# Piece-contiguous weight layout, later caching of the first mixer's weights, a skewed first norm, and LN statistics and a conv tap on ScalarE

## The chip, the cores and the metric

The kernel runs on 8 cores of one Trainium2 chip. Each core works on its own 4096 of the 32768 tokens, and the cores do not talk to one another. The metric is device time in microseconds (us) of the slowest core. Engines are named as in the profile: PE (TensorE matmul), PEld (its weight loads), DVE (VectorE), ACT (ScalarE), POOL (GpSimd), SP (SyncE, which here only issues DMA).

Executions come in two states. In the fast state the times of one kernel mostly lie within some tenths of a per cent. In the slow state the cores of one die, or of both, show a lower granted clock, and the run is per cents longer.

## The reference, cut to what matters

```python
# Layer 0: RMSNorm -> one input projection, split between mixer A and mixer B
z = h @ w_in                                   # 1024 -> 2560 columns
a = a_val * sigmoid(a_gate)                    # A: gated linear unit
a = causal_depthwise_conv(a, conv_a_w) + conv_a_b      # 31 taps, 512 channels
a = silu(layer_norm(a, ln_a_g, ln_a_b))        # LN over the 512 channels
bo = b_gate * causal_depthwise_conv(c_gate * b_val, conv_b_w)   # B: 3 taps
h = h + concatenate([a, bo]) @ w_out           # 1024 -> 1024
h = h + squared_relu_mlp(rms_norm(h), w1, w2)  # 1024 -> 4096 -> 1024
# Layer 1: a gMLP mixer, then another squared-ReLU MLP; at the end a final RMSNorm
```

Inputs and weights are float32. The kernel computes its matmuls in bfloat16.

## The kernel before: the parts that the argument touches

Each core runs four macro tiles (called tiles 0 to 3 below) of 1024 tokens through both layers. "Mixer 0" is layer 0's mixer, "mixer 1" layer 1's. The weights pass through the core as 45 *pieces* of 1024x512 per tile, in a ring of four 1 MB slots. In tile 0 a piece is read from DRAM in float32 and cast to bfloat16 by the DMA (2 MB read, 1 MB written, issued by POOL). When its last reader is done with the slot, the bfloat16 piece is stored to a DRAM cache (1 MB, issued by ACT). Tiles 1 to 3 load all pieces from the cache (1 MB, ACT's queue).

```python
def issue(i, gate=()):
    ...
    if i >= NPIECE:                                    # tiles 1 to 3: from the cache
        src = wcache[i % NPIECE].rearrange("p (kc n) -> p kc n", kc=8)
        P.op("act", lambda e, s=s, src=src: e.dma_start(out=ring[s][:], in_=src),
             reads=[("wc", i % NPIECE)], writes=[("w", s)], dma=f"v{s}")
        return
    src = W[wn][r0:r0 + 1024, c0:c0 + 512].rearrange("(kc p) n -> p kc n", p=128)
    P.op("pool", lambda e, s=s, src=src: e.dma_start(out=ring[s][:], in_=src),   # casts
         reads=list(gate), writes=[("w", s)], dma=f"w{s}")
```

Mixer 0 needs its data in another partition layout twice. The output of A's gated unit goes through a DRAM scratch, `scr_a`, into the tile `A4` that feeds the convolution (four stores of 256 KB and four reloads, issued by SP). The result after LN goes through `scr_s` into `mixT`, which feeds the output projection. The convolution runs on PE against expanded weights `cw`, which `gen_cw` builds on DVE during tile 0's first matmuls. LN's statistics are a matmul with ones and six small operations; then, per block m of four, POOL subtracts the mean, DVE multiplies by the inverse deviation, ACT applies SiLU, and SP stores.

```python
small("dve", lambda e: e.tensor_scalar(out=ln_mean.v, in0=banks[b][:, 0:TP], scalar1=1.0 / 512, ...))
small("dve", lambda e: e.tensor_scalar(out=ln_t.v, in0=banks[b][:, TP:2 * TP], scalar1=1.0 / 512, ...))
small("dve", lambda e: e.tensor_tensor(out=ln_rstd.v, in0=ln_mean.v, in1=ln_mean.v, op=ALU.mult))      # L832
small("dve", lambda e: e.scalar_tensor_tensor(out=ln_t.v, in0=ln_t.v, scalar=LN_EPS, in1=ln_rstd.v,
                                              op0=ALU.add, op1=ALU.subtract))                          # L834
small("act", lambda e: e.activation(out=ln_rstd.v, in_=ln_t.v, func=AF.Sqrt))
small("dve", lambda e: e.reciprocal(out=ln_rstd.v, in_=ln_rstd.v))
for m in range(4):
    for eng, t_, op in (("pool", ln_mean, ALU.subtract), ("dve", ln_rstd, ALU.mult)):   # L843
        lazy(m, eng, ...)
    ...                                        # SiLU on ACT, store to scr_s[m], two reloads into mixT
```

The first norm of tile 0 runs tile by tile: statistics and reciprocal root, scaling on ACT or DVE in turn, eight transposes on PE, a copy with the norm's gain on DVE (`xnT`), then matmuls. The other norms are hidden behind matmuls of earlier stages.

Of the kernel before, what the change touches and what calls it, by code (L numbers as in the profile page):

```python
# [18 lines left out]
NTB = 8  # L19
NSLOT = 4  # L20
# [163 lines left out]
GRAN = 256  # L184
B_COLS = [("c", 0), ("v", 0), ("c", 1), ("v", 1), ("g", 0), ("c", 2), ("v", 2), ("g", 1), ("c", 3), ("v", 3), ("g", 2), ("g", 3)]
# [30 lines left out]
def build_program(n_mt=4):  # L216
# [4 lines left out]
    W = {  # L221
        "ev_w_in": dram("ev_w_in", [1024, 2560]), "ev_w_out": dram("ev_w_out", [1024, 1024]),
        "od_w_in": dram("od_w_in", [1024, 2048]), "od_w_out": dram("od_w_out", [1024, 1024]),
        "w1_0": dram("w1_0", [1024, 4096]), "w1_1": dram("w1_1", [1024, 4096]),
        "w2_0": dram("w2_0", [4096, 1024]), "w2_1": dram("w2_1", [4096, 1024]),
    }
# [10 lines left out]
    with contextlib.ExitStack() as es:  # L237
# [14 lines left out]
        mhalf = sb("mhalf", [128, 1])  # L252
        st = sb("st", [128, 64])
# [78 lines left out]
        def issue(i, gate=()):  # L332
            if i >= len(pieces):
                return
            assert i == issued[0]
            issued[0] += 1
            wn, r0, c0 = pieces[i]
            s = i % NSLOT
            if i >= NPIECE:
                src = wcache[i % NPIECE].rearrange("p (kc n) -> p kc n", kc=8)  # L340
                P.op("act", lambda e, s=s, src=src: e.dma_start(out=ring[s][:], in_=src),
                     reads=[("wc", i % NPIECE)], writes=[("w", s)], dma=f"v{s}")
                return
            src = W[wn][r0:r0 + 1024, c0:c0 + 512].rearrange("(kc p) n -> p kc n", p=128)
            P.op("pool", lambda e, s=s, src=src: e.dma_start(out=ring[s][:], in_=src),
                 reads=list(gate), writes=[("w", s)], dma=f"w{s}")

        def take(expect):
# [5 lines left out]
            if i < NPIECE < len(pieces):  # L354
                wb_left[s] = [2, i]
# [4 lines left out]
        def used(s):  # L360
# [3 lines left out]
            if wb_left[s][0] == 0:  # L364
                i = wb_left.pop(s)[1]
                dst = wcache[i].rearrange("p (kc n) -> p kc n", kc=8)
                P.op("act", lambda e, s=s, dst=dst: e.dma_start(out=dst, in_=ring[s][:]),
                     reads=[("w", s)], writes=[("wc", i)], dma=f"wb{s}")
# [16 lines left out]
        def h_keys(tb):  # L385
            return [("h", tb, 0), ("h", tb, 1)]

        P.op("sp", lambda e: e.dma_start(out=sm[:], in_=smallp), writes=[("sm",)], dma="c0")
        issue(0)
        small("pool", lambda e: e.memset(identf.v, 0.0), [], identf.k())  # L390
        small("pool", lambda e: e.affine_select(out=identf.v, in_=identf.v, pattern=[[-1, 128]],
                                                compare_op=ALU.not_equal, fill=1.0, base=0,
                                                channel_multiplier=1), identf.k(), identf.k())
        small("pool", lambda e: e.tensor_copy(out=ident[:], in_=identf.v), identf.k(), [("ident",)])
        small("pool", lambda e: e.memset(mhalf[:], -0.5), [], [("mhalf",)])
        for tb in range(NTB):
            load_x(0, tb)
            if tb == 0:
                P.op("sp", lambda e: e.dma_start(out=wexp.v, in_=wexp_d.rearrange("p (g u) -> p g u", g=NG)),
                     writes=wexp.k(), dma="c1")  # L400
# [11 lines left out]
        def gen_cw(g):  # L412
            small("dve", lambda e: e.tensor_tensor(
# [124 lines left out]
        def norm_to_xnT(nidx):  # L538
# [5 lines left out]
            def tile(tb):  # L544
                if tb + 1 < NTB:
                    stat_tb(c0, tb + 1)
                    rstd_aff(c0, tb + 1)
                rstd_sqrt(c0, tb)
                rstd_rcp(c0, tb)
                xn_op(c0, tb, "act" if tb % 2 == 0 else "dve")  # L550
# [590 lines left out]
```

## Time and profile before

| | before |
|---|---|
| median of three runs | 2734.26 us (2732.64 to 2736.68) |
| PE busy in the profiled execution | 2645.3 of 2730.4 us |
| of the rest: before t = 200, that is in tile 0's mixer 0 | 58.6 us |
| mean granted clock, core 2 | 0.994 |

PE is the bound, and nearly all that can be won by moving work is the PE idle time at the start. These are lines of the page of the profile before: the span, busy time by engine, then the span cut into 40 slices, where each digit is the busy share of one slice in tenths (PEclk is the clock granted to PE, DMA the share of 16 DMA engines), then one DMA queue (packets, MB, share of 16 engines), and one group of DMA issues (count, size, median time to landing).

```profile
span 2730.4 us, 39950 instructions; the slowest of 8 cores (2717.9 to 2730.4 us)
...
PE 2645.3 (97%) x13400; PEld 1260.4 (46%) x13400; DVE 1061.8 (39%) x1957; ACT 907.5 (33%) x1627; POOL 689.0 (25%) x676
...
PE   5889999999999999999999999999999999999998
...
PEclk9989999999999999999999999999999999999999
DMA  8668765887652112123244122123316222212212
...
q0 software_dynamic: 46800, 47.19, 12.5%
...
ring<-wcache ACTq DMA_DIRECT2D x135, 1024.0 KB, 5.7
```

The first four digits of PE are the loss. DMA is busiest in the same first quarter, which is tile 0, where every piece is cast from float32 and stored to the cache. The queue q0 carries those cast loads: 47.19 MB in 46800 packets, about 1 KB each.

The view of waits says what PE waited for, over the whole span (line and tile that PE was about to run, what ended the wait, us in total, times, longest).

```profile
PE bank L500 <- ACT xn_tm L487: 19.8, 2, 16.9
PE bank L631 <- DVE Z L913: 10.9, 4, 2.9
PE bank L631 <- DMA Z<-scr_s: 9.5, 1, 9.5
PE bank L784 <- DMA Z<-scr_a: 8.9, 3, 5.0
...
PE bank L681 <- DVE Z L913: 8.1, 4, 2.3
```

L500 is the transposes of the first norm, L784 the convolution, L631 the output projection, and L913 DVE's multiply by mixer B's gate, which frees a PSUM bank or completes `mixT`. Of the waits on `scr_a` and `scr_s`, 8.9 and 9.5 us, all but 0.55 us lies in tile 0. The two lines with L913 make 19.0 us, or 4.75 us in each of the four mixers 0.

DVE's part of the LN statistics in tile 1, from the timeline of DVE in the kernel before (start, duration, line, operation, destination and source, shapes, count; in brackets the idle time before and what ended it):

```profile
785.31 2.53 DVE L832 TENSOR_TENSOR Z<-Z 128x256 f32<-128x256 f32 x1
787.95 2.38 DVE L834 SCALAR_TENSOR_TENSOR Z<-Z 128x256 f32<-128x256 f32 x1
...
796.77 3.32 DVE L904 SCALAR_TENSOR_TENSOR Z<-Z,sm 128x768 f32<-128x768 f32 x4
```
The timeline of POOL in the same stretch of the kernel before:

```profile
785.21 9.64 POOL L843 TENSOR_TENSOR Z<-Z 128x1024 f32<-128x1024 f32 x4 [10.68 <-DVE Z L828]
```

Two DVE operations on 128x256 elements take 2.53 and 2.38 us. The operations of that size just before them, which read PSUM, take 0.42 and 0.41 us. The two slow ones end as POOL's subtractions end (9.64 us for four, so 2.41 us each, from 785.21 on). The Trainium skill, "SBUF — State Buffer", section "Who interferes with whom", says that a DVE instruction with two SBUF inputs and a GpSimd instruction that reads SBUF cannot run together, and that the one to issue second blocks until the first is done. This trace agrees.

The load on the machine at that time, from the view of windows (stretch, length, busy time with count of PE, PEld, DVE, ACT and POOL, then clock, DMA share, GB/s):

```profile
735.00:765.00 30.00, 30.00 (x152) 14.52 (x150) 11.27 (x18) 7.55 (x14) 0.00 (x0) 1.00 0.70 216
```

The first `scr_a` store of tile 1 was issued at 745.39, and the reload that waits for it at 755.59, so it took 10.2 us. PE was busy for all 30 us, because the matmuls of mixer A covered it.

### The profile page before, as it was taken

The numbers are of one execution on the slowest core, as the hardware profiler recorded it, in microseconds if no ns is written. First come the engines' busy times: TensorE is split into PE (matmuls) and PEld (weight loads), VectorE is DVE, ScalarE is ACT, GpSimd is POOL, SyncE is SP. The second block draws the span as 40 slices with busy tenths as digits, with TensorE's granted clock in tenths as the row PEclk, the third lists the DMA queues.
The fourth block names the chain that finished last, engine by engine and source line by source line (L and its number), as shares of the span: only waits on it lengthen the run. The fifth ranks groups of instructions, "written<-read, shape, count | busy, mean of one in ns | idle before, by whom it ended". The sixth has DMA issues, their size and how long they took to land.

```text
span 2730.4 us, 39950 instructions; the slowest of 8 cores (2717.9 to 2730.4 us)
## 1 busy us (share of the span) xinstructions
PE 2645.3 (97%) x13400; PEld 1260.4 (46%) x13400; DVE 1061.8 (39%) x1957; ACT 907.5 (33%) x1627; POOL 689.0 (25%) x676
## 2 busy tenths in 40 slices
PE   5889999999999999999999999999999999999998
PEld 2434444444454444444454444454445444444443
DVE  3841226422464223731157321561135721265223
ACT  3332126423344114523333312552333422164112
POOL 0115321423212222223301223123320033203222
PEclk9989999999999999999999999999999999999999
DMA  8668765887652112123244122123316222212212
GB/s 163 133 143 163 163 136 124 177 182 144 211 174 74 73 65 89 64 95 122 78 166 143 62 93 78 47 83 119 107 72 209 78 93 78 78 54 86 78 62 93
DMA packets 122407, 303.87 MB, mean 111 GB/s; under 512 B 22880, under 2 KB 85344, under 8 KB 99040
## 3 DMA queue, kind: packets, MB, share of 16 engines
q10 hardware_dynamic: 25920, 188.76, 18.7%
q0 software_dynamic: 46800, 47.19, 12.5%
q1 hardware_dynamic: 49488, 65.38, 7.5%
q8 instruction: 112, 1.84, 0.3%
q14 instruction: 87, 0.71, 0.1%
HBM read 276.13 MB, written 72.35 MB: 128 GB/s over the span
## 4 chain that ended last, share of the span: by engine, by line
PE 90%; DVE 3%; DMA 3%; issue 3%; ACT 0%; SPq 0%; DVEq 0%; ACTq 0%
PE bank L694 43%; PE bank L681 41%; PE bank L500 2%; PE bank L784 2%; PE bank L631 1%; DMA scr_s<-Z 1%; DMA scr_a<-Z 1%; DVE Z L904 1%; PE bank L1014 1%; DMA Z<-scr_a 0%; DMA h<-x 0%; DVE Z L832 0%; DVE Z L834 0%; DVE Z L913 0%; DVE Z L901 0%
## 5 line engine op out<-in xcount | busy, mean ns | idle before, releaser
L681 PE MATMUL bank<-xnT,ring 128*128 128x512 bf16 x5888 | 1292.1, 380 | 13.1 <-DVE Z L913 8.1
L694 PE MATMUL bank<-ring,Z 128*128 128x512 bf16 x4928 | 1080.9, 379 | 0.1
L702 DVE TENSOR_TENSOR h<-bank,h 128x512 f32<-128x512 f32 x640 | 439.5, 690 | 1397.1 <-PE bank L694 1352.3
L681 PEld LDWEIGHTS bank<-xnT,ring 128*128 128x128 bf16 x5888 | 573.6, 98 | 699.2 <-issue 24.6
L733 POOL TENSOR_TENSOR Z<-Z 128x512 bf16<-128x512 f32 x512 | 531.2, 1039 | 1108.2 <-ACT Z L731 1108.1
L694 PEld LDWEIGHTS bank<-ring,Z 128*128 128x128 bf16 x4928 | 479.3, 98 | 565.4 <-issue 0.6
L731 ACT ACTIVATE Z<-bank 128x512 f32<-128x512 f32 x512 | 304.1, 597 | 1109.1 <-PE bank L681 1080.6
L472 ACT ACTIVATE junk<-h 128x1024 bf16<-128x1024 f32 x136 | 141.8, 1043 | 147.5 <-DVE h L702 80.2
L487 ACT ACTIVATE xn_tm<-h,st 128x1024 bf16<-128x1024 f32 x100 | 114.6, 1146 | 116.0 <-DVE st L519 100.5
L512 DVE TENSOR_TENSOR xnT<-bank,sm 128x1024 bf16<-128x1024 bf16 x96 | 115.5, 1216 | 19.1 <-PE bank L500 19.1
L694 PE MATMUL bank<-ring,xnT 128*128 128x512 bf16 x512 | 115.1, 379 | 0.0
L500 PE MATMUL bank<-ident,xn_tm 128*128 128x128 bf16 x928 | 70.7, 223 | 33.0 <-ACT xn_tm L487 19.8
L500 PEld LDWEIGHTS bank<-ident,xn_tm 128*128 128x128 bf16 x928 | 60.4, 99 | 61.5 <-issue 43.6
L986 POOL TENSOR_TENSOR st<-st,mhalf 128x1 f32<-128x1 f32 x32 | 17.6, 549 | 236.5 <-DVE st L984 236.5
L784 PE MATMUL bank<-Z,cw 128*128 128x256 bf16 x576 | 67.2, 280 | 8.9 <-DMA Z<-scr_a 8.9
L694 PEld LDWEIGHTS bank<-ring,xnT 128*128 128x128 bf16 x512 | 49.4, 98 | 56.7
L526 ACT ACTIVATE st<-st 128x1 f32<-128x1 f32 x160 | 31.0, 194 | 130.8 <-DVE st L519 108.7
L1022 DVE SCALAR_TENSOR_TENSOR Z<-bank,sm,biasT 128x128 f32<-128x128 f32 x256 | 68.9, 339 | 12.8 <-PE bank L1014 12.4
L631 PE MATMUL bank<-ring,Z 128*128 128x512 bf16 x192 | 47.2, 409 | 20.4 <-DVE Z L913 10.9
L784 PEld LDWEIGHTS bank<-Z,cw 128*128 128x128 bf16 x576 | 57.6, 100 | 18.8 <-issue 9.9
L1027 POOL TENSOR_TENSOR Z<-Z 128x512 bf16<-128x512 f32 x44 | 50.4, 1158 | 62.7 <-DVE Z L1022 62.7
L968 DVE TENSOR_TENSOR Z<-bank,cst 128x512 f32<-128x512 f32 x64 | 44.1, 689 | 40.2 <-PE bank L694 32.5
(88 smaller groups left out, 983.2 us busy)
## 6 DMA issues: line engine op xcount, KB each, us to landing
ring<-wcache ACTq DMA_DIRECT2D x135, 1024.0 KB, 5.7
wcache<-ring ACTq DMA_DIRECT2D x45, 1024.0 KB, 9.2
h<-x SPq DMA_DIRECT2D x32, 512.0 KB, 11.1
ring<-w_0 POOLq DMA_DIRECT2D x16, 1024.0 KB, 13.9
ring<-w_1 POOLq DMA_DIRECT2D x16, 1024.0 KB, 19.2
y<-Z SPq DMA_DIRECT2D x32, 512.0 KB, 3.1
Z<-x SPq DMA_DIRECT2D x24, 512.0 KB, 6.9
ring<-ev_w_in POOLq DMA_DIRECT2D x5, 1024.0 KB, 16.7
```

The lines of the kernel that those rows point to most:

```text
L472: small("act", lambda e: e.activation(out=junk[:], in_=ap, func=AF.Square, accum_out=st[:, c0 + tb:c0 + tb + 1]), keys, [("st", c0 + tb), ...
L487: small("act", lambda e: e.activation(out=out, in_=ap, func=AF.Copy, scale=col), keys + [("st", c0 + 8 + tb)], okeys)
L500: r = e.transpose(tbk[:, kc * 128:(kc + 1) * 128], xt[:, kc * 128:(kc + 1) * 128], ident[:])
L512: small("dve", lambda e: e.tensor_tensor(out=xnT[:, :, tb * 128:(tb + 1) * 128], in0=tbk.rearrange("p (k n) -> p k n", k=8), in1=gcol.unsq ...
L631: r = e.matmul(banks[b][:], lhsT=lhs(kc, tb), rhs=ring[slot][:, kc, :], start=(kc == 4), stop=(kc == 3))
L681: r = e.matmul(banks[b][:], lhsT=ring[slot][:, kc, m * 128:(m + 1) * 128], rhs=xnT[:, kc, s * 512:(s + 1) * 512], start=(kc == 0), stop=(k ...
L694: r = e.matmul(banks[b][:], lhsT=lhs(kc, tb), rhs=ring[slot][:, kc, :], start=(kc == 0), stop=(kc == 7))
L702: small("dve", lambda e: e.tensor_tensor(out=h[:, tb, d * 512:(d + 1) * 512], in0=banks[b][:], in1=h[:, tb, d * 512:(d + 1) * 512], op=ALU ...
L731: small("act", lambda e, b=b, rb=rb: e.activation(out=rb.v, in_=banks[b][:], func=AF.Relu), [("ps", b)], rb.k())
L733: small("pool", lambda e, rb=rb, hq=hq, c=c, s=s: e.tensor_tensor(out=hq.v[:, c, s * 512:(s + 1) * 512], in0=rb.v, in1=rb.v, op=ALU.mult), ...
L784: r = e.matmul(banks[b][:, half_ * TP:(half_ + 1) * TP], lhsT=cw[:, g, L * 128:(L + 1) * 128], rhs=A4.v[:, g, HB - L:HB - L + TP], start=( ...
L1022: r = e.scalar_tensor_tensor(out=sv.v[:, j * 128:(j + 1) * 128], in0=banks[b][:, j * 128:(j + 1) * 128], scalar=sm[:, SM_LNGV + g:SM_LNGV ...
```

## The change

Five things to shorten the 58.6 us at the start and the small waits in each mixer 0:

1. The host lays each piece out contiguously, so that what a partition gets of it is one run of 16 KB in float32, where it was eight runs of 2 KB. Piece 0 is split into two halves, and the first half is loaded alone, so that the first matmul group can start sooner.
2. The seven pieces of mixer 0 are cached one tile later. Their cache stores leave tile 0 and happen in tile 1, which therefore casts these seven pieces from float32 again.
3. The first norm is skewed: the statistics of a tile run ahead of the scaling of the tile before, all scaling is on ACT, the transposes come one step later, and three of the `gen_cw` go to POOL.
4. In the LN statistics the square goes to ACT, one operation is dropped and one reads PSUM.
5. The last tap of mixer B's 3-tap convolution goes from DVE to ACT, for three of its four blocks.

```diff
+NSPLIT = 1
+NLATE = 7
 ...
-    W = { "ev_w_in": dram("ev_w_in", [1024, 2560]), ... }
+    W = {n: dram(n, [128 * (k // 1024) * (c // 512), 4096]) for n, (k, c) in WSHAPE.items()}
 ...  (issue)
-            if i >= NPIECE:
-                src = wcache[i % NPIECE].rearrange("p (kc n) -> p kc n", kc=8)
-                P.op("act", lambda e, s=s, src=src: e.dma_start(out=ring[s][:], in_=src), ...
+            if i // NPIECE > cache_mt(i):          # cache_mt: 1 for pieces 0 to NLATE-1, else 0
+                P.op("act", lambda e, s=s, i=i: e.dma_start(out=ring_flat(s), in_=wcache[i % NPIECE]), ...
                 return
-            src = W[wn][r0:r0 + 1024, c0:c0 + 512].rearrange("(kc p) n -> p kc n", p=128)
+            q = (r0 // 1024) * (WSHAPE[wn][1] // 512) + c0 // 512
+            src = W[wn][q * 128:(q + 1) * 128, :]
+            if wn == "ev_w_in" and q < NSPLIT:     # two halves, each with its own key
+                ...
 ...  (first norm)
             stats(0)
+            for tb in range(4):
+                stats(tb + 1)
+                scale(tb)
+                if tb > 0:
+                    tr_op(nidx, tb - 1)
+                gen_cw(3 + tb)
+            tr_op(nidx, 3)
 ...  (LN statistics)
-                small("dve", ... out=ln_t.v, in0=banks[b][:, TP:2 * TP], scalar1=1.0 / 512 ...)
-                small("dve", ... out=ln_rstd.v, in0=ln_mean.v, in1=ln_mean.v, op=ALU.mult ...)
-                small("dve", ... out=ln_t.v, in0=ln_t.v, scalar=LN_EPS, in1=ln_rstd.v ...)
-                small("act", ... activation(out=ln_rstd.v, in_=ln_t.v, func=AF.Sqrt) ...)
+                small("act", ... activation(out=ln_t.v, in_=ln_mean.v, func=AF.Square) ...)
+                small("dve", ... scalar_tensor_tensor(out=ln_t.v, in0=banks[b][:, TP:2 * TP], scalar=1.0 / 512,
+                                                      in1=ln_t.v, op0=ALU.mult, op1=ALU.subtract) ...)
+                small("act", ... activation(out=ln_rstd.v, in_=ln_t.v, func=AF.Sqrt, bias=leps[:, 0:1]) ...)
 ...  (mixer B)
+            def tap2(m):
+                if m < 3: small("act", ... activation(out=cv, in_=src, func=AF.Copy, scale=w2) ...)
+                else:     small("dve", ... tensor_scalar(out=cv, in0=src, scalar1=w2 ...) ...)
 ...  (start)
-        for k in range(1, NSLOT):
-            issue(k, h_keys(6) if k == 1 else [("w", k - 1)])
+        late_part.pop()(1, h_keys(1))              # the second half of piece 0
+        gen_cw(14, "pool")
+        issue(1, h_keys(4))
+        gen_cw(15, "pool")
+        gen_cw(13, "pool")
+        issue(2, h_keys(7))
+        issue(3, wk(2))
+        for g in range(3):
+            gen_cw(g)
```

## The prediction

> **What bounds it now.** PE is busy 2645 of 2730 us (engine table of the page), granted clock 0.994. The windows view places the 86 us left: 58.6 before t = 200 (tile 0's mixer 0), about 5 in each mixer 0 of macro tiles 1 to 3, 10 in the tail. DMA is 0.6 to 0.8 busy for the first 700 us (slices), but PE is full from t = 200, so that costs nothing there.
>
> The 58.6, from PE's timeline: 16.9 before the first transpose; transposes and four lone groups until continuous matmuls at 49.4; 5.0 and 3.4 waiting for A4 before the convolution (scr_a stores take 15.5, 5.4, 8.1 us; 4.2 is the median); about 24 between the convolution's end (99.4) and the out projection (164.8), 9.5 of it a reload of scr_s behind stores of 14.7 and 13.1 us that overlap w_0 loads and cache stores.
>
> **What the change does.**
> 1. Contiguous pieces. A cast load is now 1024 packets of 1 KB at 98 ns (6.3 us of all 16 DMA engines). Plain 8 KB packets take 309 ns; reading 2 MB so would be about 5 us (estimate). It counts only before t = 165.
> 2. Seven cache stores move from tile 0 to tile 1, which also gets seven 2 MB cast loads in place of cached ones. Clears tile 0's scr traffic, burdens tile 1's, where A4 and mixT have few us to spare: 0 to 6 us lost.
> 3. First norm. Bound by x landing (x1 at 13.9, x3 at 19.3, beside the whole piece) and a 3.9 us ACT-DVE-PE round trip per tile. Half a piece first and skewing make it about 3.1 (ACT: 1.23 statistics, 0.2, 1.15 scaling, hand-over). First matmul group at 24 to 28 (was 31.2), continuous at 38 to 42.
> 4. LN statistics. Two DVE operations of 128x256 take 2.53 and 2.38 us, a similar one 0.42: each ends as a POOL subtraction (2.35 to 2.53 us) ends. The Trainium skill, "SBUF — State Buffer", says a DVE operation with two SBUF inputs and a GpSimd operation reading SBUF exclude each other; the trace agrees. One goes to ACT, one reads PSUM: 4 us off the chain, but later multiplies then meet the remaining subtractions, so perhaps 1.5 stays.
> 5. Tap 2 on ACT: 0.75 us off DVE, three times per mixer. With 4, the 4.65 us of PE waits on DVE's gate multiply (1.95 + 2.70) falls to 1 to 2.
>
> **Sum.** Head -9; A4 waits -7; tile-0 LN and B stage -15; less cold clock -2; tiles 1 to 3 -9 for DVE, +3 for DMA. Tail, MLP, mixer 1 unchanged. About -37: **2697 us**, range 2684 to 2713. Over 2% faster (under 2680) needs 55 of the 86 us, and head and tail keep nearly 40: chance 0.05; within 2%: 0.94; slower: 0.01.
>
> **What would show it.** First group and continuous PE at those times; no scr_a wait above 1 us in tile 0; MLP from about 163 (was 198); tile-0 scr_s stores under 8 us; LN statistics 4 us sooner; small gate waits later; cache stores at 740 to 840.
>
> **What would make it wrong.** Large weight packets holding up the 256 and 512 B packets of the scr stores (the skill's "DMA: Bandwidth & Descriptors": queues take turns by packet); gen_cw on DVE and POOL excluding each other in the head; tile 1 stalling 10 us as tile 0 did.

## More of the kernel before

Last, tile 1: the conversion of layout before the convolution, from the timeline of SP in the kernel before.

```profile
725.36 16.89 SPq L626 DMA_DIRECT2D y<-Z  x6
745.39 0.38 SPq L770 DMA_DIRECT2D scr_a<-Z  x1
755.59 0.53 SPq L773 DMA_DIRECT2D Z<-scr_a  x1
```

## The result, and the profile after

| | before | after |
|---|---|---|
| median of all runs of this comparison | 2735.47 us (2732.64 to 2741.85, 4 runs) | 2738.48 us (2734.84 to 3117.39, 4 runs, one slow) |
| ratio of fast runs | | 1.0006, 95% interval 0.9982 to 1.003 |

A ratio in this document is the mean time of one kernel's fast runs over that of the other's of the same rounds, so it is not quite the ratio of the medians that are quoted. (Here it also counts a fifth run of the changed kernel, 2740.43 us.) The change is worth nothing, at a time outside the predicted range of 2684 to 2713 us.

To see where the expected 37 us went, the span is cut into stages. A stage begins when a given matmul starts, counted from the first one; both kernels do the same 13,400 matmuls, and on PE in the same order but for some transposes at the start. The times below are worked out from the start times in the traces: medians over the cores whose trace holds all 13,400 records (six of eight in both kernels).

```
stage                                        before    after   change   predicted
start to the 97th matmul (PE continuous)       49.0     45.6     -3.4      -9
tile 0: mixer A's matmuls                      23.0     23.1     +0.1  }   -7 (waits
tile 0: convolution                            22.0     21.5     -0.5  }       for A4)
tile 0: mixer B, LN                            49.4     45.4     -4.0  }  -15
tile 0: output projection, first 70            24.6     18.0     -6.6  }
rest of tile 0                                561.1    562.1     +1.0       0
tile 1: mixer A's matmuls                      23.6     23.6      0.0
tile 1: wait for A4, convolution               16.6     36.0    +19.4      +3 (DMA)
tile 1: mixer B                                43.8     41.9     -1.9  }   -9 (DVE),
tile 2: mixer 0                               103.9    102.1     -1.8  }    tiles 1 to 3
tile 3: mixer 0                               104.0    103.5     -0.5  }
span (median of these cores)                 2724.1   2724.1      0.0
```

The stages that were to be shortened won 18.6 us together (3.4, 0.4, 10.6 and 4.2), about half of what was expected, and one stage of tile 1 lost 19.4. These are the lines of the page after that answer to those of before.

```profile
span 2733.6 us, 39966 instructions; the slowest of 8 cores (2720.4 to 2733.6 us)
...
PE 2652.5 (97%) x13400; PEld 1262.6 (46%) x13400; DVE 1045.0 (38%) x1930; ACT 927.2 (34%) x1647; POOL 686.5 (25%) x689
...
PE   5999999999989999999999999999999999999998
...
PEclk9999999999989999999999999999999999999999
DMA  7456565677863212123244122123326222212212
...
q0 software_dynamic: 11360, 54.53, 12.0%
...
ring<-wcache ACTq DMA_DIRECT2D x128, 1024.0 KB, 5.0
```

PE is fuller in the second and third slice, and an 8 has appeared in the 12th (751 to 820 us), with an 8 in the clock of the same slice. The DMA row is lower than before in slices 1 to 5 (tile 0's start), and higher in slices 11 to 13 (8, 6, 3 where it was 6, 5, 2). Seven loads have left the cache group (x135 became x128) and are cast loads in tile 1. The packets of q0 are now nearly five times as large on the mean: 54.53 MB in 11360, where it was 47.19 MB in 46800.

The waits of PE, from the view of waits after:

```profile
PE bank L524 <- ACT xn_tm L511: 26.1, 6, 15.7
PE bank L820 <- DMA Z<-scr_a: 22.7, 3, 17.6
PE bank L667 <- DVE Z L959: 11.7, 4, 3.0
...
PE bank L667 <- DMA Z<-scr_s: 1.4, 1, 1.4
...
PE bank L717 <- DVE Z L959: 0.4, 1, 0.4
```

The wait for `scr_s` has shrunk from 9.5 to 1.4 us. The gate waits have shrunk from 19.0 to 12.1 us (11.7 and 0.4). The wait for `scr_a` has grown from 8.9 to 22.7 us, and 17.6 of it is a single wait. The same store in tile 1, from the timeline of SP after:

```profile
726.72 0.38 SPq L806 DMA_DIRECT2D scr_a<-Z  x1
759.43 0.54 SPq L809 DMA_DIRECT2D Z<-scr_a  x1
```
The view of windows after, for the same stretch of time as before:

```profile
735.00:765.00 30.00, 12.36 (x58) 5.89 (x57) 2.48 (x4) 1.68 (x3) 1.06 (x2) 0.72 0.85 192
```

The first `scr_a` store of tile 1 is issued at 726.72, and its reload at 759.43: 32.7 us, where it took 10.2 us. PE is busy for 12.36 of 30 us, and the granted clock falls to 0.72. The DMA share is 0.85. From 675 us on, POOL issued cast loads at 675.77 (two halves), 688.54, 716.20 and 717.90, and ACT cache stores at 675.02, 691.06 (two), 722.82 and 730.12; more cast loads follow at 741.32 and 746.86.

DVE around the LN statistics in tile 1, from the timeline of DVE after:

```profile
789.38 0.42 DVE L868 SCALAR_TENSOR_TENSOR Z<-bank,Z 128x256 f32<-128x256 f32 x1 [0.62 <-ACT Z L866]
...
794.01 2.97 DVE L878 TENSOR_TENSOR Z<-Z 128x1024 f32<-128x1024 f32 x1
...
796.97 5.45 DVE L950 SCALAR_TENSOR_TENSOR Z<-Z,sm 128x768 f32<-128x768 f32 x4
```
The timeline of POOL after, in the same stretch:

```profile
788.91 6.98 POOL L878 TENSOR_TENSOR Z<-Z 128x1024 f32<-128x1024 f32 x3 [10.66 <-DVE Z L864]
```

The statistics no longer block: the operation on PSUM takes 0.42 us. But the subtractions still have to run, and DVE now meets them later: the first LN multiply (L878) takes 2.97 us, where it took 1.50, and the four tap operations (L950) 5.45 us, where they took 3.32. From the first operation after the statistics' matmul to the end of the taps DVE needs 14.1 us (788.34 to 802.42), where it needed 15.5 (784.64 to 800.09). Some 1.4 us stay, but not all of it belongs to the statistics, because one tap operation has also left this stretch. With the tap back on DVE and the changed statistics kept (e11 below), the stretch takes 14.7 us (794.99 to 809.68). So about 0.8 us is due to the statistics and 0.6 us to the tap.

And the head, where the time to continuous PE fell by 3.4 us only, from the timeline of DVE after:

```profile
14.11 3.27 DVE L437 TENSOR_TENSOR cw<-Z 128x1152 bf16<-128x1152 f32 x1
...
21.25 5.16 DVE L437 TENSOR_TENSOR cw<-Z 128x1152 bf16<-128x1152 f32 x1
```
The timeline of POOL after, in the head:

```profile
14.02 2.14 POOL L437 TENSOR_TENSOR cw<-Z 128x1152 bf16<-128x1152 f32 x1
...
20.98 4.21 POOL L437 TENSOR_TENSOR cw<-Z 128x1152 bf16<-128x1152 f32 x2
```
And the timeline of ACT after, in the head:

```profile
26.64 1.15 ACT L511 ACTIVATE xn_tm<-h,st 128x1024 bf16<-128x1024 f32 x1 [4.09 <-DVE st L555]
```

A `gen_cw` on DVE takes 1.34 to 1.35 us alone. The one at 14.11 began just after POOL's at 14.02 and took 3.27 us. The one at 21.25 began after POOL's pair at 20.98 and took 5.16 us. A small reciprocal of the norm is queued behind it on DVE, so ACT stands idle for 4.09 us before the scaling at 26.64.

### The profile page after: what moved, and what is told of

Same layout as the page of the kernel before. It is cut to its first block, busy times and chain, and to the rows that moved or that the text cites. A ratio compares the mean times of both kernels' runs of the same rounds, so it can differ in the third digit from the quotient of the medians.

```text
span 2733.6 us, 39966 instructions; the slowest of 8 cores (2720.4 to 2733.6 us)
## 1 busy us (share of the span) xinstructions
PE 2652.5 (97%) x13400; PEld 1262.6 (46%) x13400; DVE 1045.0 (38%) x1930; ACT 927.2 (34%) x1647; POOL 686.5 (25%) x689
## 3 DMA queue, kind: packets, MB, share of 16 engines
q0 software_dynamic: 11360, 54.53, 12.0%
## 4 chain that ended last, share of the span: by engine, by line
PE 90%; DMA 3%; DVE 3%; issue 2%; ACT 1%; SPq 0%; DVEq 0%; ACTq 0%
PE bank L730 43%; PE bank L717 41%; PE bank L820 2%; PE bank L524 2%; DMA scr_a<-Z 2%; PE bank L667 2%; DVE Z L950 1%; DMA scr_s<-Z 1%; PE bank L1060 1%; DMA Z<-scr_a 0%; DMA h<-x 0%; DVE Z L933 0%; DMA Z<-scr_s 0%; DVE Z L959 0%; ACT Z L914 0%
## 5 line engine op out<-in xcount | busy, mean ns | idle before, releaser
L820 PE MATMUL bank<-Z,cw 128*128 128x256 bf16 x576 | 68.9, 284 | 24.7 <-DMA Z<-scr_a 22.7
L1032 POOL TENSOR_TENSOR st<-st,mhalf 128x1 f32<-128x1 f32 x32 | 17.6, 549 | 238.8 <-DVE st L1030 238.8
L667 PE MATMUL bank<-ring,Z 128*128 128x512 bf16 x192 | 48.4, 417 | 13.1 <-DVE Z L959 11.7
## 6 DMA issues: line engine op xcount, KB each, us to landing
h<-x SPq DMA_DIRECT2D x32, 512.0 KB, 10.6
ring<-w_0 POOLq DMA_DIRECT2D x16, 1024.0 KB, 12.2
```

The lines of the kernel that those rows point to most:

```text
L667: r = e.matmul(banks[b][:], lhsT=lhs(kc, tb), rhs=ring[slot][:, kc, :], start=(kc == 4), stop=(kc == 3))
L820: r = e.matmul(banks[b][:, half_ * TP:(half_ + 1) * TP], lhsT=cw[:, g, L * 128:(L + 1) * 128], rhs=A4.v[:, g, HB - L:HB - L + TP], start=( ...
```

## The experiments

**Theories for tile 1's 19.4 us.** OVERLAP (in the records below also LATE): the seven late pieces' transfers, casting loads and cache stores, take DMA time while the small `scr_a` stores need it, and any way of having fewer of them in flight removes the stall. Rival 1, PACKET: the new layout's 8 KB packets make each small packet wait longer, so that small pieces of the same bytes would cure it. The Trainium skill, "DMA: Bandwidth & Descriptors", section "Queues, rings and completion order", says that a DMA engine takes turns between queues by whole packets, which speaks for this rival. Rival 2, QUEUE: the store sits behind eight y stores of 512 KB on SP's own queue. **Theory for the head:** LOCK, DVE's and POOL's `gen_cw` exclude each other; the rival is that x or the first half piece lands late.

### e1_late0: the change without the late caching

```diff
-NLATE = 7
+NLATE = 0
```

> The changed kernel with the first seven pieces cached in tile 0 again, all else as changed. Theory LATE (moving cast loads and cache stores of mixer 0 into tile 1 makes its 17.6 us wait for A4): tile 1's convolution waits under 2 us, as before; tile 0 gives back 3 to 10 us because cache stores collide with its scr traffic again; time about 2723 to 2731 us. Rival SKEW (the stall comes from the other parts, for instance the head start of the whole pipeline or the contiguous pieces alone): the stall in tile 1 stays above 10 us and the time near 2738.

Fast runs 2719.23 to 2729.94 us; ratio 0.9954 (0.9925 to 0.9982). The stage of tile 1 fell from 36.0 to 16.8 us, and tile 0's output projection rose from 18.0 to 24.5 us. Two lines of its view of waits of PE:

```profile
PE bank L667 <- DMA Z<-scr_s: 8.0, 1, 8.0
PE bank L820 <- DMA Z<-scr_a: 7.5, 4, 5.8
```

The late caching makes the stall of tile 1, and it also makes the gain at tile 0's output projection: without it an 8.0 us wait for `scr_s` is back there. As a trade it loses about 13 us net (19.2 less 6.5). The other four parts of the change together win about half a per cent. Even so, e1's median of 2723.79 us lies above the predicted range, so the late caching is not the whole of the miss.

### e2_pack1k: the same layout with small packets

Every run of 512 elements is padded by 16 in DRAM, so that a cast load is again made of 1 KB packets, with all else as in the change.

```diff
+CH = 512
+CP = CH + 16
+WROW = (4096 // CH) * CP
 ...
-            P.op("pool", lambda e, s=s, src=src: e.dma_start(out=ring_flat(s), in_=src), ...
+            P.op("pool", lambda e, s=s, src=src: e.dma_start(
+                out=ring_flat(s).rearrange("p (k n) -> p k n", n=CH),
+                in_=src.rearrange("p (k n) -> p k n", n=CP)[:, :, 0:CH]), ...
```

> The changed kernel with each 512-element run of a piece padded by 16 elements in DRAM, so cast loads go in 1 KB packets again, from nearly contiguous memory; caching stays late. Theory PACKET (8 KB cast packets of 625 ns and more take turns with the packets of the y and scr_a stores and hold them up): tile 1's wait for A4 falls from 17.6 us to under 5, time about 2722 to 2728. Rival VOLUME (the same bytes in the same stretch, whatever the packets): the wait stays above 12 us and the time within 5 us of 2738.

Fast runs 2731.84 to 2737.22 us; ratio 0.9993 (0.9956 to 1.0031). The stage of tile 1 took 33.4 us, 2.6 less than 36.0. PACKET explains 2.6 of 19 us and falls as the main cause. The packets of the cast loads took 98 ns for 1 KB and 625 ns for 8 KB (of the result), from the records of the trace: for one piece, with 1024 or 128 packets on 16 engines, 6.3 or 5.0 us of all engines (both from median packet times). The small packets thus also cost more engine time, so the effect of packet size by itself may be somewhat larger than 2.6 us. But e3 below stalls as well, and its cast packets are of 1 KB too.

### e3_before_late7 and e4_before_layout: one part alone, on the kernel before

```diff
 # e3_before_late7
-            if i >= NPIECE:
+            if i // NPIECE > (1 if i % NPIECE < NLATE else 0):        # NLATE = 7
 ...
-            if i < NPIECE < len(pieces):
+            if i // NPIECE == (1 if i % NPIECE < NLATE else 0) and i + NPIECE < len(pieces):
```

> The kernel before with one change only: seven pieces cached in tile 1. LATE and VOLUME: tile 1's A4 wait grows from 0 to above 10 us while tile 0 gains 8 to 12 us in the stage after the convolution (no cache stores beside scr_s); time within 8 us of 2735. LATE and PACKET (1 KB packets here): tile 1 waits under 5 us, so tile 0's gain stays: about 2722 to 2728 us.

```diff
 # e4_before_layout
-            src = W[wn][r0:r0 + 1024, c0:c0 + 512].rearrange("(kc p) n -> p kc n", p=128)
+            q = (r0 // 1024) * (WSHAPE[wn][1] // 512) + c0 // 512
+            src = W[wn][q * 128:(q + 1) * 128, :]
```

> The kernel before with one change only: contiguous pieces (8 KB cast packets). If the layout is worth the 1 to 2 us a piece that I predicted, tile 0's scr stores get shorter and its MLP starts 3 to 8 us sooner: about 2728 to 2732 us. If PACKET holds, larger packets delay x and scr stores in tile 0 and it starts no sooner or later: 2735 or more. Tile 1 unchanged in both.

e3 alone: fast runs 2740.40 to 2747.68 us, ratio 1.0024 (0.9999 to 1.0049); the output projection of tile 0 fell by 8.7 us (24.6 to 15.9) and the stage of tile 1 rose by 15.2 us (16.6 to 31.8). So the stall needs neither the new layout nor the other parts. e4 alone: fast runs 2734.59 to 2738.34 us, ratio 1.0000 (0.9974 to 1.0026); its profile fell in the slow state of die 1, so its stages were read from three cores of die 0: none moved by more than 3.6 us, and their sum did not move. The layout by itself is worth nothing here.

### e5_loads_only and e6_stores_only: which of the transfers

```diff
 # e5_loads_only: tile 0 stores the pieces as before, tile 1 still casts them
-            if i // NPIECE == cache_mt(i) and i + NPIECE < len(pieces):
+            if i < NPIECE and i + NPIECE < len(pieces):
 # e6_stores_only: tile 1 loads from the cache, and stores the seven pieces once more
-            if i // NPIECE > cache_mt(i):
+            if i >= NPIECE:
 ...
-            if i // NPIECE == cache_mt(i) and i + NPIECE < len(pieces):
+            if i < NPIECE + NLATE and i + NPIECE < len(pieces):
```

> The changed kernel, but the seven cache stores are made in tile 0; tile 1 still makes its seven cast loads of 2 MB. Theory LOADS (the cast loads make tile 1's wait): its conv stage (16.8 us when nothing is late, 36.0 as changed, medians over the cores) stays above 30. Rival STORES (the seven stores make it): the stage falls under 22. If both share it, between 22 and 30. Tile 0's out projection goes back to about 24 us from 18. Time 2735 to 2745 under LOADS, 2722 to 2730 under STORES.

> The other half: tile 1 loads its first seven pieces from the cache, as if nothing were late, and stores them to the cache once more. LOADS: tile 1's conv stage under 22 us, time within 4 us of the run with nothing late (2723.8). STORES: the stage above 30 and the time near 2740.

e5 had two fast runs (2735.39 and 2746.39 us) and no ratio; e6 had two (2733.97 and 2741.90 us), ratio 1.0019 (0.9989 to 1.0048). In e5 the stage of tile 1 took 29.0 us, 12.2 above e1's 16.8; in e6 23.1 us, 6.3 above. Together that is 18.5 us, against 19.2 us with both (36.0 less 16.8). Both profiles had a disturbed pair of cores (0 and 1 at a clock of 0.983 in e5, 2 and 3 at 0.984 to 0.986 in e6); without them the stages are 30.3 and 23.7 us, and the reading is the same. Loads and stores each add their part. No single kind of transfer is to blame; the amount of traffic is.

### e7_y_on_act: the y stores on another queue

```diff
-            P.op("sp", lambda e: e.dma_start(out=dst, in_=ob.v), reads=ob.k(), dma=f"out{tb % 4}")
+            P.op("act" if mt == 0 else "sp", lambda e: e.dma_start(out=dst, in_=ob.v), ...
```

> The changed kernel with tile 0's eight y stores issued from ACT's queue instead of SP's, so that tile 1's first scr_a store is not queued behind them. Theory QUEUE (the store of 32.7 us waits in the SP queue behind y stores that the cast loads hold up): the first store takes under 15 us and tile 1's conv stage falls from 36 us to under 24, time about 2722 to 2730. Rival SATURATION (all 16 DMA engines are full, whichever queue): the stage stays above 30 and the time within 5 us of 2738.

Fast runs 2733.44 and 2734.35 us; ratio 1.0004 (0.998 to 1.0028). The first `scr_a` store took 15.0 us instead of 32.7, but the second now took 16.3 us, and the stage lasted 34.0 us against 36.0. Two of 19 us: QUEUE falls too. The Trainium skill, "DMA: Bandwidth & Descriptors", section "Issuing engines are not separate DMA queues", says that transfers from all issuing engines run on the same 16 DMA engines, so that another issuer saves only issue time. This run agrees: the wait moved from the first store to the second.

### e14_t1_gate: the same transfers, later

This is the direct test of OVERLAP. Nothing is removed from the change. The cast loads of pieces 2 to 5 of tile 1 are only issued when `A4` has been reloaded.

```diff
         def release(i):
+            if NPIECE + 2 <= i + NSLOT <= NPIECE + 5:
+                deferred.append(i + NSLOT)
+                return
             issue(i + NSLOT)
 ...
+                    if mt == 1 and m == 3:
+                        for k in deferred:
+                            issue(k, [("A4", g) for g in range(12, 16)])
```

> The changed kernel as it is, but tile 1's casting loads of pieces 2 to 5 are issued only when its A4 has been reloaded. Theory OVERLAP (loads hurt because they run beside the scr_a traffic; two cache stores still do): tile 1's conv stage falls from 36.0 to 20 to 24 us and nothing later grows by more than 2, time 2722 to 2728. Rival TOTAL (the same bytes cost PE the same time wherever they stand in mixer 0): the stage falls but tile 1's B stage or out projection grows by about as much, time 2734 or more.

Fast runs 2729.16 to 2734.97 us; ratio 1.0005 (0.9992 to 1.0018). The stage of tile 1 fell from 36.0 to 16.6 us. The timeline of SP in its trace, in tile 1:

```profile
698.25 24.71 SPq L667 DMA_DIRECT2D y<-Z  x8
724.66 0.38 SPq L811 DMA_DIRECT2D scr_a<-Z  x1
729.70 0.53 SPq L814 DMA_DIRECT2D Z<-scr_a  x1
```
The timeline of PE in the same trace, after the convolution of tile 1:

```profile
766.78 7.76 PE L722 MATMUL bank<-xnT,ring 128*128 128x512 bf16 x24 [7.58 <-DMA ring<-ev_w_in]
```

The same store, behind the same eight y stores, now takes 5.0 us (724.66 to 729.70) instead of 32.7. So the cast loads in flight beside it are what makes this stage stall. Two cache stores are still issued beside it (at 720.76 and 728.06), and without the loads they do no harm here. But the bytes still have to come: PE waits 7.58 us for the pieces of mixer B, that stage grows by 8.4 us (41.9 to 50.3), and the output projection by 11.5 us (19.2 to 30.7). The three together come to 97.6 us, against 97.1 in the change and 79.5 in the kernel before. Moving the loads inside mixer 0 only moves the stall; mixer 0 has no room for them. In the words of the expectation this second half is its rival TOTAL, and not OVERLAP, which expected no later stage to grow by more than 2 us: in this run the overlap decided which stage stalls, and not how much is lost.

### e8_late0_head: the head without `gen_cw` on POOL

```diff
 # on e1_late0
         late_part.pop()(1, h_keys(1))
-        gen_cw(14, "pool")
         issue(1, h_keys(4))
-        gen_cw(15, "pool")
-        gen_cw(13, "pool")
         issue(2, h_keys(7))
 ...     (the three are made on DVE later, between mixer A's first groups)
```

> The kernel with nothing late (2723.8 us) with its three gen_cw on POOL moved to DVE after the first norm. Theory LOCK (POOL's gen_cw and DVE's exclude each other; two DVE ones took 3.27 and 5.16 us where 1.34 is usual, and held the reciprocal that the fourth tile's scaling waits for): all DVE gen_cw take 1.35 us, the first matmul group starts at 24 to 27 us instead of 30, continuous matmuls 3 to 5 us sooner than 45.2 (median over the cores), time about 2719. Rival XLOAD (x still arrives too late): the start moves less than 1.5 us.

Fast runs 2718.51 to 2733.40 us; ratio 0.9986 (0.9953 to 1.0019), with cores 0 and 1 at a clock of 0.984 in the profiled run. The timeline of DVE in its trace, in the head:

```profile
20.14 1.35 DVE L437 TENSOR_TENSOR cw<-Z 128x1152 bf16<-128x1152 f32 x1
```
The timeline of PE in the same trace, at its first matmul group:

```profile
25.60 5.80 PE L717 MATMUL bank<-xnT,ring 128*128 128x512 bf16 x16 [1.48 <-DVE st L555]
```

All `gen_cw` on DVE now take 1.35 us where in the change they had taken up to 3.27 and 5.16. The first matmul group starts at 25.9 us (median of the cores), 3.4 earlier than e1's 29.3, and PE is continuous from 43.4, 1.8 earlier than e1's 45.2. LOCK is shown for the first group, with the size of the loss. The rest of the head is another thing: on ACT a cache store of piece 0 waited for its late half and held up the queue for 1.66 us, and the copy of the last transposes' result waited behind a DVE operation of mixer A.

### e11_late0_tap_dve: the tap back on DVE

```diff
 # on e1_late0
-                if m < 3:
+                if m < 0:
```

> The kernel with nothing late, with the conv tap back on DVE; the LN statistics stay changed. Mixer 0 of tiles 2 and 3 took 103.9 and 104.0 us before and 101.7 and 103.2 in that kernel. If the tap brings about 0.9 us a tile (0.74 + 0.5 - 0.3, from DVE's waits in the trace), they become about 102.6 and 104.1 and tile 1's B stage 42.8 (41.9); if the tap is worth what I predicted (2.2), 103.9 and above; if nothing, no change. Time within 3 us of 2724.

Fast runs 2724.12 to 2747.66 us; ratio 1.0022 (0.9963 to 1.0082), unclear. Tile 0's mixer B took 47.1 us against 45.6. Mixer B alone took 43.1, 43.1 and 43.5 us in tiles 1, 2 and 3, against 41.9 in each in e1, and these stages differ by less than 0.1 us between the cores that were read, although cores 2 to 5 of this profile were at a clock of 0.982 to 0.986. So the tap is worth 1.2 to 1.6 us in mixer B of every tile. Over the whole of mixer 0, tiles 2 and 3 show nothing of it (101.5 with the tap on DVE against 101.7, and 102.9 against 103.2): in both of these tiles the output projection behind mixer B is shorter with the tap on DVE, by more than 1 us in the median; it also differs by 1.4 to 1.8 us between the cores of e1. Mixer B took 43.8, 43.7 and 43.8 us in the kernel before, so the LN statistics are left with 0.6, 0.6 and 0.3 us of it, by elimination; this was not measured alone.

The traces of e1 and e11 show one more block that the prediction did not foresee. In e1, on core 0, a DVE copy of 128x4 elements, which reads SBUF once, took 2.31 us instead of 0.16 (776.20 to 778.51); it ended as POOL's fourth subtraction did (778.48). In e11 the tap of the first block, a multiply by one factor per partition, took 2.24 us instead of 0.75 while POOL subtracted.

### e9_dram_copy, e10_copy_gate and e12_copy_fixed: caching by another way

The stores can also leave tile 0's mixer 0 without a second cast into the ring: POOL copies the piece from DRAM to DRAM, float32 to bfloat16, at a later time in tile 0. e9 does this for seven pieces, on e8, and also issues the transposes of the first norm's last tiles earlier. e10 adds gates: tile 0's loads of pieces 4, 5 wait for `A4`, and 7, 8 for `mixT`. e12 is e10 with two faults of e9 mended: the halves of the first copy no longer wait for one another, and the copies come later, over mixer 1 and the second MLP.

```diff
 # e9_dram_copy
+COPY_AT = (9, 13, 17, 21, 25, 29, 33)
+        def copy_piece(j): ...
+            P.op("pool", lambda e: e.dma_start(out=wcache[j], in_=src), writes=[("wc", j)], dma="cc")
         def release(i):
             issue(i + NSLOT)
+            if i in COPY_AT:
+                copy_piece(COPY_AT.index(i))
 ...
+                if mt == 0 and (m, s) == (1, 0):
+                    pump(NTB)                              # the transposes earlier
 # e10_copy_gate
-                    release(b_pc[b_rel[0]][0])
+                    release(b_pc[b_rel[0]][0], mixT.k(3 * T, 4 * T) if mt == 0 and b_rel[0] > 0 else ())
 ...
-                        release(a_pc[m // 2][0])
+                        release(a_pc[m // 2][0], [("A4", g) for g in range(4 * m, 4 * m + 4)] if mt == 0 else ())
 # e12_copy_fixed
-COPY_AT = (9, 13, 17, 21, 25, 29, 33)
+COPY_AT = (24, 27, 30, 33, 36, 39, 41)
 ...  (and each copy has a key and a semaphore of its own)
```

> Built from what the runs showed: the first seven pieces get to the cache by casting copies from DRAM to DRAM, issued between releases of ring slots in tile 0's MLP and mixer 1, so neither mixer 0 has cache stores and tile 1 loads from the cache; gen_cw on DVE alone as in e8; the last transpose of the first norm one step sooner. If the two places where the stores hurt are the only ones, tile 0's out projection is near 18 us (24.5 with stores), tile 1's conv stage near 17, continuous matmuls at 39 to 42 us: 2708 to 2714 us. If the copies disturb the weight loads of the full-PE stretch, the stretch from MLP to tile 1 (561 us) grows by more than 3.

> e9, and in tile 0 the casting loads of pieces 4 and 5 wait until A4 of their half is reloaded, and those of pieces 7 and 8 until mixT is. If the rest of tile 0's waits for A4 and mixT comes from these loads sharing the DMA engines with the scr traffic, the conv stage falls from 21 to 23 us to about 18 and the out projection to about 16: 2701 to 2708 us. If not, the stages stay, and weights that come too late may add waits.

> e10 with its two faults mended: the two halves of piece 0's copy no longer wait for one another, and the seven DRAM to DRAM copies are issued in mixer 1 and the second MLP of tile 0. If e10's loss (the stretch from MLP to tile 1 grew from 561 to 580.6 us) came from POOL blocked in that wait and from copies beside the busiest weight stretch, the stretch returns to 561 to 564 and tile 0 keeps e10's head of 140.8 us up to the end of the out projection: 2694 to 2702 us. If copies disturb the weights wherever they are, the stretch stays above 568 and the time above 2704.

e9: 2721.22 to 2737.98 us, ratio 0.9992 (0.9946 to 1.0037), unclear. The head shortened to 40.2 us and the output projection to 20.2, but the rest of tile 0 grew by 9.7 us over the change (571.8). Two suspects were visible: the two halves of the first copy had one key, so POOL waited 16.65 us between them while its other work stood, and the copies ran beside the MLP's own loads. e10: 2723.77 to 2750.34 us, ratio 1.0022 (0.9933 to 1.0111), unclear. Its gates brought the convolution of tile 0 to 16.0 us, from 22.7, and the output projection to 16.8. So the wait for `A4` in tile 0 is an overlap as well, with the loads of pieces 4 and 5. It is one with cache stores too: e13 below has the same gates with all cache stores in tile 0, and its convolution takes 21.0 us; e12 and e16, without the stores of pieces 0 and 1 there, take 16.8 and 16.2. Taking away the stores alone (e9: 22.7) does not help; both have to go. But the rest of tile 0 cost 580.6 us in e10. e12: 2717.10 to 2725.55 us, ratio 0.9971 (0.9959 to 0.9983), with that stage still at 578.3, where its expectation was 561 to 564. Mending both suspects won only 2.3 us over e10, so neither the shared key of the halves nor the place of the copies is the main cause of the loss there.

### e13_late0_head_gate and e15_clean_gate: the gates without copies

```diff
 # e13_late0_head_gate: e8 with e9's earlier transposes and e10's gates, no copies
 # e15_clean_gate: the gate of pieces 7 and 8 gets a key that nothing else uses
-                            [("scrs", m)], mixT.k(m * T + q * 512, m * T + (q + 1) * 512), dma=f"t{m}")
+                            [("scrs", m)], mixT.k(...) + ([("td", m)] if mt == 0 else []), dma=f"t{m}")
 ...
-                    release(b_pc[b_rel[0]][0], mixT.k(3 * T, 4 * T) if mt == 0 and b_rel[0] > 0 else ())
+                    release(b_pc[b_rel[0]][0], [("td", 3)] if mt == 0 and b_rel[0] > 0 else ())
```

> Nothing late and no copies (all cache stores in tile 0), with e8's gen_cw, the earlier last transpose, and e10's gates on the casting loads of tile 0. If tile 0's waits for A4 and mixT come from the casting loads, this does nearly as well as e10 there: conv stage 16 to 18 us, out projection 17 to 19, time 2696 to 2704. If the cache stores matter as much (they did by half in tile 1: 6.3 of 18.5 us), the out projection stays at 20 to 23 and the time 2702 to 2712.

> e13 with its gate on mixT mended: in e10, e12 and e13 the gate read mixT, so a later write of the MLP's hidden tile over that region waited for a weight load (10.9 us on POOL, 6.5 on PE in e13's trace). Now the gate reads a key of its own. If that false wait was the loss in the stretch from MLP to tile 1, it goes from 568.3 to 561 to 563 with tile 0's head unchanged (146 us to the end of the out projection): median span over the cores about 2699, time 2699 to 2707. If the weights themselves come too late for an MLP that starts sooner, the stretch stays above 566.

e13: fast runs 2709.85, 2712.76 and 2740.82 us, ratio 0.9965 (0.9925 to 1.0005). Its profile had cores 2 and 3 at a clock of 0.97, so the others were read. The rest of tile 0 took 568.3 us, with no copy in it. The timeline of POOL on its undisturbed core 0:

```profile
245.98 8.01 POOL L769 TENSOR_TENSOR Z<-Z 128x512 bf16<-128x512 f32 x8 [10.28 <-DMA ring<-w]
```
The timeline of PE on the same core:

```profile
250.25 11.99 PE L730 MATMUL bank<-ring,Z 128*128 128x512 bf16 x47 [3.44 <-POOL Z L769]
```

The gate reads `mixT`. The MLP's hidden tiles lie in the same memory, so POOL's first write there must wait until that gated load has landed: 10.28 us on POOL, and 3.44 us on PE behind it (3.4 to 5.4 us on the four undisturbed cores that were looked at). In e15, where the gate has its own key, that stage is back at 561.1 us on die 0 (its cores 6 and 7 were at a clock of 0.985). The borrowed key thus cost 7.2 us. e12 has it too; the other 10 us of e12's loss (578.3 less 568.3) go with the copies, by difference only. e15's fast runs spread from 2703.82 to 2739.86 us, ratio 0.9963 (0.9904 to 1.0022).

### e16_clean_copy2: a version that beats both

e12 with e15's clean gate, and with only pieces 0 and 1 cached by copies, during mixer 1; the other five of mixer 0 are stored from the ring in tile 0 as before.

```diff
-NLATE = 7
-COPY_AT = (24, 27, 30, 33, 36, 39, 41)
+NLATE = 2
+COPY_AT = (24, 27)
```

> e12 with the same mended gate, and only pieces 0 and 1 copied DRAM to DRAM (both issued in mixer 1), so that the two cache stores beside tile 0's scr_a traffic are gone and few copies burden the second MLP. If those two stores are what keeps e13's conv stage at 21.0 against e12's 16.8, it is 16 to 18 here; with the MLP stretch at 561 to 564 the time is 2695 to 2704. If the copies cost PE time anyway, the stretch grows by more than 4 and the time is that of e15 or above.

Fast runs 2706.60 to 2708.57 us (two more were slow), ratio 0.9912 (0.9894 to 0.9929): faster than the kernel before by 0.9%. By stage, against the kernel before (computed as above; medians of single stages do not add up exactly):

```
stage                                        before      e16   change
start to the 97th matmul                       49.0     40.6     -8.4
tile 0: mixer A's matmuls                      23.0     22.3     -0.7
tile 0: convolution                            22.0     16.2     -5.8
tile 0: mixer B, LN                            49.4     45.9     -3.5
tile 0: output projection, first 70            24.6     16.8     -7.8
rest of tile 0                                561.1    566.7     +5.6
tile 1: A4, convolution, mixer B               60.4     58.9     -1.5
tile 2 and tile 3: mixer 0                    207.9    205.4     -2.5
span (median of these cores)                 2724.1   2698.4    -25.7
```

The 5.6 us in the rest of tile 0 is one 5.5 us wait of PE on POOL in the second MLP, after a copy. There POOL had stood for 12.48 us until a cache store landed, before it could issue the next weight load; that the copy delayed this store is not shown. e15, which copies nothing, does not have it, and the four die-0 cores of its profile were as fast (2696.3 to 2704.2 us). Whether e15 or e16 is the better kernel stays open: e15's fast runs spread too far.

## Why the prediction was wrong, point by point

The prediction was about -37 us (its terms as written add up to -39), and the runs showed none of it.

The step that failed is item 2 of the prediction, "burdens tile 1's, where A4 and mixT have few us to spare: 0 to 6 us lost". The term in the sum was +3, and it measured +19.4 us. These 16 us more account for less than half of the distance between -37 and the result: the gains, predicted at 40 us (the cold clock's 2 left out), came to 18.6. The points below say which of them failed. For tile 1, the mechanism was named, also in the last paragraph ("tile 1 stalling 10 us as tile 0 did"), but the size was guessed and not costed. It could have been costed from the trace of before. Seven cast loads at the 5 us that item 1 estimates are 35 us of all 16 DMA engines. The seven cached loads that they replace are 17 us (128 packets at 309 ns over 16 engines are 2.5 us each), and the seven cache stores add about 17 again, if their packets cost the same. That is an estimate of 35 us more DMA time, to be fitted into a mixer 0 of about 103 us whose DMA share was already 0.70 in the critical stretch. e1 shows that the late caching is the cause, e5 and e6 that loads and stores share it, e14 that their overlap with the small stores decides where PE stalls, and e2 and e7 that neither the packets' size nor the queue is more than 2 or 3 us of it.

- **"Head -9": measured -3.4.** The sequence was estimated from ACT's durations alone, 3.1 us per tile. The prediction's last paragraph named "gen_cw on DVE and POOL excluding each other in the head" as a risk and gave it no time. It cost 3.4 us at the first group (e8). Another part was the order of the last transposes: with both mended, e9's head is 40.2 us and e16's 40.6, inside the 38 to 42 that was predicted.
- **"A4 waits -7": measured -0.4** (mixer A and convolution of tile 0 together). The failed step is item 2's "Clears tile 0's scr traffic". It clears cache stores, but the `scr_a` stores of tile 0 also overlap the cast loads of pieces 4 and 5, which stay. A wait of 4.91 us for `scr_a` stayed there, where the prediction expected none above 1. Gating those two loads took 6.7 us off e9's convolution (e10).
- **"Tile-0 LN and B stage -15": measured -10.6** (-4.0 and -6.6). The direction and the order of size were right, and e1 shows that 6.5 us of it belong to the late caching. One `scr_s` store of tile 0 still took 9.3 us, where the prediction expected all to be under 8.
- **"Tiles 1 to 3 -9 for DVE": measured -4.2** (-1.9, -1.8, -0.5). The prediction's caution, "later multiplies then meet the remaining subtractions, so perhaps 1.5 stays", had the right mechanism, but only about 0.8 us stays on DVE from the statistics and 0.3 to 0.6 us per tile on PE (e11). The step that failed is "the 4.65 us of PE waits on DVE's gate multiply (1.95 + 2.70) falls to 1 to 2". The first of the two waits did go (8.1 to 0.4 us in four mixers), but the second, before the output projection, did not (10.9 to 11.7 us), so 3.0 us per mixer were left. In tile 2 of the trace after, PE's last matmul of mixer B ends at 1488.86, and PE waits 2.84 us, while DVE is still at the last block's taps (3.32 us, to 1489.66) and gate multiplies.
- **"Less cold clock -2": did not come.** Mean clocks went from 0.993 to 0.995 down to 0.990 to 0.993 over the cores; in the stall of tile 1 it was 0.72.
- **"It counts only before t = 165"** of the layout was right in tendency: alone, it is worth nothing (e4).
- **"MLP from about 163 (was 198)":** continuous matmuls of the first MLP began at 177.6 us in the profiled core. By the medians of the stages 14.4 us were won up to there, and all of it was lost again in tile 1, up to t = 763.

What is not settled: what exactly is exhausted in the stall of tile 1. The DMA share was 0.85 and not 1, so a limit of the DRAM side or of single engines may play a part; no run tells these apart.

## What to carry to other kernels

Before moving transfers from one stage to another, cost them in the destination as carefully as in the source: add their DMA time to that stage's share, and look which small transfers on the critical path they will meet. Work that DVE and POOL are to do side by side must be checked for two SBUF inputs on DVE, also where it is only filler work, because a blocked filler holds up the small operations queued behind it. One SBUF input is no safeguard: a copy with one was held for 2.31 us in e1. When a load is gated to keep it out of the way, gate it on a key of its own: a borrowed one orders it against things that have nothing to do with it.

## What the Trainium skill lacked or had wrong

- "DMA: Bandwidth & Descriptors" gives advice for the bandwidth of large transfers ("Rules for kernel authors": at least 1 MiB per DMA) and tells how engines take turns, but it has no figure for how long a small transfer on the critical path takes beside large ones: the same 256 KB store took 32.7 us beside casting loads of 2 MB and 5.0 us when four of these were held back (e14).
- The same page has no cost for a DMA that casts. The packets took 98 ns for 1 KB and 625 ns for 8 KB of result, where a plain 8 KB packet took 309 ns (medians).
- The same page, "SWDGE vs HWDGE vs iDMA", puts a packet at "≤4096 B preferably". The traces here record packets of 8192 B, and of 32768 B in the copies from DRAM to DRAM (2.4 to 6.4 us each in e9). Whether a packet of the trace is what the page calls a packet is not shown. From its section "Queues, rings and completion order" (turns between queues by packet) one could expect much harm of such sizes to small transfers; going back to 1 KB packets won 2.6 us of 19 (e2).
- "SBUF — State Buffer", "Who interferes with whom", says that the instruction that issues second blocks until the first is done. The trace agrees (2.53 us in place of 0.42), but a DVE operation can wait for more than one: the `gen_cw` at 21.25 ended at 26.41, 1.22 us after the second of two POOL operations that followed each other (20.98 to 25.19); it had waited for both.
